# RWKV scans: outputs and next state from one product, its two uses in a step in different PSUM banks, the copy of the outputs later in the order

## The chip, the cores and the metric

The program runs on one core of one Trainium2 chip. A core has five engines that each take their own instructions in order: TensorE (PE, matrix products; its weight loads, PEld, run ahead of the products), VectorE (DVE), ScalarE (ACT), GpSimd (POOL) and SyncE (SP, which only issues DMAs here). They meet at semaphores. Products land in PSUM, which has eight banks; DVE and ACT read them from there. The metric is the device time of one execution in microseconds (us); the time given is the median of several executions.

## What is computed

Two layers of a diffusion backbone: neighbourhood attention and an expert-routed feed-forward layer, then bidirectional RWKV-7 time mixing and a second expert-routed layer, for 512 latent tokens and 256 context tokens of 1024 channels. The change concerns the RWKV scans alone: 16 heads of 64 channels, one scan forward and one backward, each with the 64x64 state S of a head carried from the context tokens into the latent ones. The outputs y of both directions are added.

```python
def _rwkv_step(S, inp):
    r, w, kk, kka, kt, v = inp
    sk = jnp.einsum('bhij,bhj->bhi', S, kk)
    S = S * w[:, :, None, :] - sk[..., None] * kka[:, :, None, :] + v[..., None] * kt[:, :, None, :]
    return S, jnp.einsum('bhij,bhj->bhi', S, r)
...
        S_f, y_f = _rwkv_scan(S0[0], (r, w[0], kk, kk * a[0], kt[0], v), False)
        S_b, y_b = _rwkv_scan(S0[1], (r, w[1], kk, kk * a[1], kt[1], v), True)
        return (S_f, S_b), (y_f + y_b, r, kt, v, g)
```

Everything is float32.

## The kernel before

The kernel goes through four phases in order: attention, first expert layer, RWKV layer, second expert layer. In the RWKV layer the 16 heads are taken in 8 pairs, and each pair has two directions z (0 forward, 1 backward): 16 directions in all. The 768 tokens are 6 tiles m of 128 tokens (0 to 3 latent, 4 and 5 context), each of two chunks u of 64 tokens. A scan does not go token by token: `rw_dir_in` and `rw_invert` turn a chunk into matrices, and `rw_dir_out` then needs one small recurrence per chunk.

For each chunk there is a matrix FT (128 rows; per head 128 columns) and a matrix Z (128 rows; per head 64 columns). Rows 0 to 63 of Z are the chunk's values v, which a DMA brings (`states`); rows 64 to 127 are the state that comes from the chunk before. Columns 64 to 127 of FT give the next state, columns 0 to 63 the chunk's outputs. Of context tiles no outputs are needed.

The functions in `rw_dir_out`, by the order in which `run` calls them for the i-th tile of the direction's order:

- `chain(i, us[0])`: for each of the two heads one product of FT's columns 64 to 127 with Z, into the lower half (partitions 64 to 127) of a tile of the pool `ps_ch`, which has one PSUM bank (tile name `ch`, L1537). DVE multiplies the result by the decay and writes it into the next chunk's Z (L1540).
- `transition(order[i + 1])`: the FT of both chunks of the next tile: products of FR with QF into the pool `ps_mm` (three banks, tile name `mm`, L1520), copied into FT by ACT (L1522) and DVE (L1523, L1527).
- then, after a yield, `chain(i, us[1])`, in the same bank `ch`;
- `solve(order[i + 2])`: products of RHS with TB (L1504), into `mm`, copied into QF by ACT (L1508);
- `outputs(m)`, for latent tiles: four products of FT's columns 0 to 63 with Z, two per chunk, the chunk u in partitions 64u to 64u+63 of one `mm` tile (L1550). For z = 0 ACT copies them to y (tile name `yg`, L1552); for z = 1 DVE adds them to y (L1554).

FT tiles come from the pool `rp`, four in turn. Each product of the program is float32 and shows in the trace as two pairs of LDWEIGHTS and MATMUL, so the two heads of a chain product are x4 in a row of the trace, and the four products of `outputs` are x8.

`weave` sets the order: it runs several generators in turn, one yield of each per step of twelve. In a scan direction's twelve steps stand the `run` of this direction, `rw_dir_in` of the direction four later (transposes L71, products L1380 and their copies BD, BKT, AT, FR, RHS), the decays of the one after (L1298), `rw_join` of the next direction (L1471, L1478), and every second direction the readout of the pair before. Under `manual_schedule` PE, DVE and ACT take the instructions in the order in which the code writes them; the DMAs and POOL's instructions are ordered by a scheduler. After the last `rw_dir_in` the output projection (`fold`, L248 to L250 into `mf`) is laid between the scans' instructions.

`later()` opens the pools `rp`, `jp` and `ro` before the first scan and fills the tiles that stay (E, TB, QF) with zeros.

Of the kernel before, what the change touches and what calls it, by code (L numbers as in the profile page):

```python
# [20 lines left out]
F32 = mybir.dt.float32  # L21
# [4 lines left out]
AF = mybir.ActivationFunctionType  # L26
ALU = mybir.AluOpType
# [4 lines left out]
P = 128  # L32
# [4 lines left out]
NLT = 4  # L37
# [1281 lines left out]
NSP = 3  # L1319
LAG = 4  # L1320
# [164 lines left out]
def rw_dir_out(S, W):  # L1485

    nc = S.nc
# [22 lines left out]
    def transition(m):  # L1510
# [3 lines left out]
        for u in us:  # L1514
# [6 lines left out]
            FT[m][u] = F = S.rp.tile([P, 2, P], F32, name="FT", bufs=4)  # L1521
# [8 lines left out]
    def chain(i, u):  # L1530
        m = order[i]
        c = 2 * m + u
        if u == us[1] and i == NT - 1:
            return
        pz = S.ps_ch.tile([P, 2, 64], F32, name="ch")
        for h in range(2):
            nc.tensor.matmul(pz[64:128, h, :], FT[m][u][:, h, 64:128], Zs[m][:, u, 64 * h:64 * h + 64],  # L1537
                             start=True, stop=True)
        dst = Zs[m][64:128, us[1], :] if u == us[0] else Zs[order[i + 1]][64:128, us[0], :]
        nc.vector.tensor_tensor(dst.rearrange("p (h i) -> p h i", h=2), pz[64:128],  # L1540
                                W.PC[64:128, :, c:c + 1].to_broadcast([64, 2, 64]), op=ALU.mult)

    def outputs(m):
        if m >= NLT:
            return
        po = S.ps_mm.tile([P, P], F32, name="mm")
        for u in range(2):
            for h in range(2):
                r = slice(64 * h, 64 * h + 64)
                nc.tensor.matmul(po[64 * u:64 * u + 64, r], FT[m][u][:, h, 0:64], Zs[m][:, u, r], start=True, stop=True)  # L1550
        if z == 0:
            nc.scalar.activation(y[:, m, :], po, AF.Copy)  # L1552
        else:
            nc.vector.tensor_tensor(y[:, m, :], po, y[:, m, :], op=ALU.add)  # L1554
# [11 lines left out]
    def run():  # L1566
        for i, m in enumerate(order):
            if i + 2 < NT:
                states(order[i + 2])
            chain(i, us[0])  # L1570
            if i + 1 < NT:
                transition(order[i + 1])
            yield
            chain(i, us[1])
            if i + 2 < NT:
                solve(order[i + 2])
            outputs(m)
            yield
# [134 lines left out]
def phase_rw(S):  # L1713
    nc, tc = S.nc, S.tc
    S.rwk = ExitStack()
    with ExitStack() as es:
# [15 lines left out]
        with ExitStack() as e1:  # L1732
# [11 lines left out]
            S.LO, S.TB, S.QF, S.qfi, S.Gs = [], [], [], 0, {}  # L1744
# [15 lines left out]
            def later():  # L1760
# [8 lines left out]
                for z in range(2):  # L1769
# [7 lines left out]
                    S.QF.append(t)  # L1777

# [133 lines left out]
```

## Time and profile before

| | us |
|---|---|
| time, median of 3 runs (lowest, highest) | 2788.53 (2783.61, 2795.34) |
| the profiled execution: its time | 2783.66 |
| the profiled execution: span from the first to the last instruction | 2781.7 |
| PE busy over the span | 2475.8 (89%) |
| DVE busy | 1337.5 (48%) |
| ACT busy | 1004.4 (36%) |
| POOL busy | 595.9 (21%) |

The first `chain` product starts at 1709.3 us of the span and the last scan ends near 2226 us. Before that lie the attention and the first expert layer, the RWKV layer's projections and the filling of its pipeline; after that the second expert layer. Busy is the time in which an engine has at least one instruction under way; PE's products overlap each other and their ends are modelled, so PE can count as busy while it loses time between products. The granted clock (PEclk) is a share of 2.4 GHz: 1.00 is that level, 0.50 is 1.2 GHz.

### The profile page before, as it was taken

How to read it: one execution, taken by the hardware profiler on the slowest of the kernel's cores; microseconds unless marked ns; L12 is line 12 of the kernel's file. 1: busy time of each engine (PE TensorE's matmuls, PEld its weight loads, DVE VectorE, ACT ScalarE, POOL GpSimd, SP SyncE). 2: the span in 40 equal slices, each digit the busy share in tenths (PEclk: the TensorE clock that was granted, in tenths of full speed). 3: DMA queues.
4: the chain of work that ended last, by engine and by line, in shares of the span. 5: the costliest groups of instructions: out<-in, count | busy, mean ns of one | idle time of the engine just before them, and what ended most of it. 6: DMA issues, size and time to landing. Idle time of an engine off the chain costs nothing. (4 is left out here: it accounts for less than half of the span.)

```text
span 2781.7 us, 43985 instructions
## 1 busy us (share of the span) xinstructions
PE 2475.8 (89%) x16803; PEld 1534.7 (55%) x16803; DVE 1337.5 (48%) x2987; ACT 1004.4 (36%) x2121; POOL 595.9 (21%) x855
## 2 busy tenths in 40 slices
PE   6999999889999999997689697999999959988887
PEld 4876778782333322333389596777778843322222
DVE  6656665551222211215978745676676762211221
ACT  3555566531110100113266535676665421000000
POOL 1110000121000000001556535665555200000000
PEclk9999999989999999998899898999999959999999
DMA  8655530329788879774157966556654279999998
GB/s 244 146 157 183 159 114 17 113 103 372 271 345 319 325 287 364 277 292 166 69 176 247 270 158 136 130 127 145 129 115 127 61 274 373 409 409 409 409 409 334
DMA packets 427521, 637.62 MB, mean 229 GB/s; under 512 B 133824, under 2 KB 301056, under 8 KB 427312
## 3 DMA queue, kind: packets, MB, share of 16 engines
q1 hardware_dynamic: 419328, 609.11, 64.7%
q0 software_dynamic: 7984, 25.70, 2.5%
q8 instruction: 134, 2.20, 0.3%
q14 instruction: 75, 0.61, 0.1%
HBM read 565.11 MB, written 53.88 MB: 223 GB/s over the span
## 5 line engine op out<-in xcount | busy, mean ns | idle before, releaser
L759 PE MATMUL P<-wm,xin 128*64 128x512 f32 x2048 | 503.3, 607 | 42.1 <-DMA wm<-in_moe_w_dram 41.9
L759 PEld LDWEIGHTS P<-wm,xin 128*64 128x64 f32 x2048 | 132.8, 137 | 369.8 <-issue 270.8
L792 PE MATMUL mm<-wm,hidT 128*64 128x512 f32 x1024 | 250.8, 601 | 20.4 <-ACT hidT L774 16.1
L768 ACT ACTIVATE hid<-P 128x512 f32<-128x512 f32 x32 | 19.1, 598 | 690.1 <-PE P L759 690.1
L803 DVE SCALAR_TENSOR_TENSOR Y<-mm,gates,gt 64x512 f32<-64x512 f32 x64 | 48.0, 750 | 320.8 <-PE mm L792 320.1
L769 DVE TENSOR_TENSOR hid<-P,hid 128x512 f32<-128x512 f32 x32 | 22.1, 692 | 371.3 <-PE P L759 371.3
L731 POOL DMA_INDIRECT xg<-xnd,ii x20 | 19.1, 956 | 808.1 <-PE tp L71 521.9
L248 PE MATMUL mm<-wh,hTh 128*128 128x256 f32 x576 | 171.6, 298 | 2.5 <-ACT hTh L542 2.5
L250 PE MATMUL mm<-wh,hTl 128*128 128x256 f32 x576 | 166.7, 290 | 1.7 <-DVE hTl L545 1.7
L249 PE MATMUL mm<-wl,hTh 128*128 128x256 f32 x576 | 166.7, 290 | 0.0
L792 PEld LDWEIGHTS mm<-wm,hidT 128*64 128x64 f32 x1024 | 69.0, 136 | 159.5 <-issue 116.4
L763 PE MATMUL Pc<-wm,xin 128*32 128x512 f32 x1024 | 147.3, 602 | 0.0
L1443 POOL TENSOR_TENSOR Wi<-Wi,Ti 112x30 f32<-112x30 f32 (+14 forms) x240 | 142.1, 592 | 18.7
L1441 POOL TENSOR_TENSOR Ti<-Wi 112x30 f32<-112x30 f32 (+14 forms) x240 | 135.8, 566 | 18.2
L248 PEld LDWEIGHTS mm<-wh,hTh 128*128 128x128 f32 x576 | 112.5, 195 | 12.7 <-issue 9.1
L250 PEld LDWEIGHTS mm<-wh,hTl 128*128 128x128 f32 x576 | 112.0, 195 | 4.2 <-DVE hTl L545 2.7
L1520 PE MATMUL mm<-FR,QF 128*128 128x128 f32 (+1 forms) x768 | 113.5, 291 | 0.4 <-ACT QF L1508 0.4
L249 PEld LDWEIGHTS mm<-wl,hTh 128*128 128x128 f32 x576 | 112.6, 196 | 1.4 <-issue 1.4
L830 DVE TENSOR_TENSOR X<-mm,X 128x512 f32<-128x512 f32 x80 | 51.9, 687 | 106.1 <-PE mm L829 105.8
L1520 PEld LDWEIGHTS mm<-FR,QF 128*128 128x128 f32 x768 | 97.1, 197 | 7.4 <-ACT QF L1508 0.9
L1508 ACT ACTIVATE QF<-mm 64x256 f32<-64x256 f32 x192 | 72.9, 379 | 66.8 <-PE mm L1504 63.1
L1523 DVE TENSOR_TENSOR FT<-mm,eye 64x128 f32<-64x128 f32 x192 | 55.9, 292 | 77.4 <-ACT FT L1522 75.4
(429 smaller groups left out, 5697.3 us busy)
## 6 DMA issues: line engine op xcount, KB each, us to landing
wm<-in_moe_w_dram SPq DMA_DIRECT2D x378, 1024.0 KB
adaw<-in_ada_w_dram SPq DMA_DIRECT2D x96, 512.0 KB
wraw<-in_na_w_qkv_dram SPq DMA_DIRECT2D x32, 256.0 KB
wm<-in_moe_w_dram POOLq DMA_DIRECT2D x6, 1024.0 KB, 11.0
pkd<-sig SPq DMA_DIRECT2D x24, 256.0 KB
pkd<-kka SPq DMA_DIRECT2D x24, 256.0 KB
pkd<-av SPq DMA_DIRECT2D x24, 256.0 KB
sig<-pkd SPq DMA_DIRECT2D x16, 384.0 KB
```

The lines of the kernel that those rows point to most:

```text
L248: S.nc.tensor.matmul(ps, xh, wh, start=(k == 0), stop=False)
L249: S.nc.tensor.matmul(ps, xh, wl, start=False, stop=False)
L250: S.nc.tensor.matmul(ps, xl, wh, start=False, stop=(k == n - 1))
L759: nc.tensor.matmul(ps[64 * hf:64 * hf + 64], xin[:, k, cl], w[:, k2, hf * 512:(hf + 1) * 512], start=st, stop=sp)
L763: nc.tensor.matmul(Pc[32 * i:32 * i + 32], xinc[:, k, cc], ws[i // 2][:, k2, (i % 2) * 512:(i % 2 + 1) * 512], start=st, stop=sp)
L792: nc.tensor.matmul(py[64 * hf:64 * hf + 64], hT[:, k % 4, k // 4, :], w[:, k2, hf * 512:(hf + 1) * 512], start=st, stop=sp)
L830: nc.vector.tensor_tensor(X[t][:, sl], ps, X[t][:, sl], op=ALU.add)
L1441: nc.gpsimd.tensor_tensor(t, W3[:, i + 1:32, i:i + 1].to_broadcast([112, n, i]), W3[:, i:i + 1, 0:i].to_broadcast([112, n, i]), op=ALU.mult)
L1443: nc.gpsimd.tensor_tensor(W3[:, i + 1:32, 0:i], W3[:, i + 1:32, 0:i], t, op=ALU.add)
L1508: nc.scalar.activation(QF[m][0:64, u], pq[64 * u:64 * u + 64], AF.Copy)
L1520: nc.tensor.matmul(pf[:, h, s0:], QF[m][:, u, h, :], rhs, start=True, stop=True)
L1523: nc.vector.tensor_tensor(F[64:128, :, 64:128], pf[64:128, :, 64:128], S.eye2[64:128, None, :].to_broadcast([64, 2, 64]), op=ALU.add)
```

## The change

Outputs and next state of a chunk now come from one product. `chain` multiplies all 128 columns of FT with Z, so that the upper half of the PSUM tile (partitions 0 to 63) holds the chunk's outputs and the lower half the next state. `outputs` is gone, with its products. The first chunk of a tile uses the bank `ch`, the second a tile of the pool `ps_mm`. `chain` returns a function that copies the outputs (ACT for z = 0, DVE for z = 1, 64 partitions at a time), and `run` calls it later: for the first chunk behind the instructions of `transition`, for the second behind those of `solve`. The last chunk of a direction, whose state nobody needs, now gets a product for its outputs. Of context tiles the outputs' half is computed too and not read. FT tiles are four fixed tiles of the pool `jp`, which `later()` fills with zeros on DVE, since context tiles leave columns 0 to 63 unwritten.

```diff
--- before.py
+++ after.py
@@ -1317,6 +1317,7 @@
 LATC = 8
 NSET = 5
 NSP = 3
+NFT = 4
 LAG = 4
 LATER, PREP0, PREP, RA, NEXT, NEXT0, RSTART, RRATE, RD = 2, 8, 6, 1.8, 5, 13, 0, 0.6, 1
 
@@ -1518,7 +1521,8 @@
                 r = slice(64 * h, 64 * h + 64)
                 rhs = W.FR[:, c:c + LATC + 1:LATC, r] if lat else W.FR[:, LATC + c, r]
                 nc.tensor.matmul(pf[:, h, s0:], QF[m][:, u, h, :], rhs, start=True, stop=True)
-            FT[m][u] = F = S.rp.tile([P, 2, P], F32, name="FT", bufs=4)
+            FT[m][u] = F = S.FT[S.fti % NFT]
+            S.fti += 1
             nc.scalar.activation(F[0:64, :, s0:], pf[0:64, :, s0:], AF.Copy)
             nc.vector.tensor_tensor(F[64:128, :, 64:128], pf[64:128, :, 64:128],
                                     S.eye2[64:128, None, :].to_broadcast([64, 2, 64]), op=ALU.add)
@@ -1530,28 +1534,26 @@
     def chain(i, u):
         m = order[i]
         c = 2 * m + u
-        if u == us[1] and i == NT - 1:
-            return
-        pz = S.ps_ch.tile([P, 2, 64], F32, name="ch")
+        if u == us[1] and i == NT - 1 and m >= NLT:
+            return lambda: None
+        pool, name = ((S.ps_ch, "ch"), (S.ps_mm, "mm"))[u != us[0]]
+        pz = pool.tile([P, 2, 64], F32, name=name)
         for h in range(2):
-            nc.tensor.matmul(pz[64:128, h, :], FT[m][u][:, h, 64:128], Zs[m][:, u, 64 * h:64 * h + 64],
-                             start=True, stop=True)
-        dst = Zs[m][64:128, us[1], :] if u == us[0] else Zs[order[i + 1]][64:128, us[0], :]
-        nc.vector.tensor_tensor(dst.rearrange("p (h i) -> p h i", h=2), pz[64:128],
-                                W.PC[64:128, :, c:c + 1].to_broadcast([64, 2, 64]), op=ALU.mult)
-
-    def outputs(m):
-        if m >= NLT:
-            return
-        po = S.ps_mm.tile([P, P], F32, name="mm")
-        for u in range(2):
-            for h in range(2):
-                r = slice(64 * h, 64 * h + 64)
-                nc.tensor.matmul(po[64 * u:64 * u + 64, r], FT[m][u][:, h, 0:64], Zs[m][:, u, r], start=True, stop=True)
-        if z == 0:
-            nc.scalar.activation(y[:, m, :], po, AF.Copy)
-        else:
-            nc.vector.tensor_tensor(y[:, m, :], po, y[:, m, :], op=ALU.add)
+            nc.tensor.matmul(pz[:, h, :], FT[m][u][:, h, :], Zs[m][:, u, 64 * h:64 * h + 64], start=True, stop=True)
+        if not (u == us[1] and i == NT - 1):
+            dst = Zs[m][64:128, us[1], :] if u == us[0] else Zs[order[i + 1]][64:128, us[0], :]
+            nc.vector.tensor_tensor(dst.rearrange("p (h i) -> p h i", h=2), pz[64:128],
+                                    W.PC[64:128, :, c:c + 1].to_broadcast([64, 2, 64]), op=ALU.mult)
+
+        def evacuate():
+            if m >= NLT:
+                return
+            o, src = y[64 * u:64 * u + 64, m, :], pz[0:64].rearrange("p h i -> p (h i)")
+            if z == 0:
+                nc.scalar.activation(o, src, AF.Copy)
+            else:
+                nc.vector.tensor_tensor(o, src, o, op=ALU.add)
+        return evacuate
 
     def prepare():
         states(order[0])
@@ -1567,14 +1569,15 @@
         for i, m in enumerate(order):
             if i + 2 < NT:
                 states(order[i + 2])
-            chain(i, us[0])
+            end = chain(i, us[0])
             if i + 1 < NT:
                 transition(order[i + 1])
+            end()
             yield
-            chain(i, us[1])
+            end = chain(i, us[1])
             if i + 2 < NT:
                 solve(order[i + 2])
-            outputs(m)
+            end()
             yield
     return prepare, run
 
@@ -1741,7 +1744,7 @@
                 setattr(S, name, opened(e1, name, b, side="right"))
             S.ps_ch = e1.enter_context(tc.tile_pool(name="ps_ch", bufs=1, space=PSUM))
             S.ps_un = ea.enter_context(tc.tile_pool(name="ps_un", bufs=2, space=PSUM))
-            S.LO, S.TB, S.QF, S.qfi, S.Gs = [], [], [], 0, {}
+            S.LO, S.TB, S.QF, S.qfi, S.FT, S.fti, S.Gs = [], [], [], 0, [], 0, {}
 
             def low(pool, i):
                 t = pool.tile([P, NT, P], F32, name=f"LO{i}")
@@ -1775,6 +1778,10 @@
                     nc.vector.tensor_copy(t[64:128, :, :, 0:64].rearrange("p u h c -> p (u h) c"),
                                           S.eye2[64:128, None, :].to_broadcast([64, 4, 64]))
                     S.QF.append(t)
+                for i in range(NFT):
+                    t = S.jp.tile([P, 2, P], F32, name=f"FT{i}")
+                    nc.vector.memset(t, 0.0)
+                    S.FT.append(t)
 
             def prep(j):
                 yield from rw_join(S, W[j])
```

The order in which the engines get the instructions, at three places. First PE, in a forward direction (z = 0), from a chain product of a context tile to the first one behind the next `outputs` (before):

```order
L1537 MATMUL ch<-Z,FT 64x64 x2
L1520 MATMUL mm<-FR,QF_14658 128x128 x4
L71 MATMUL tp<-ident,kka 128x128 x2
L71 MATMUL tp<-ident,kt 128x128 x2
L1380 MATMUL un<-BD,BKT 128x256 x2
L1537 MATMUL ch<-Z,FT 64x64 x2
L1504 MATMUL mm<-RHS,TB_14651 128x128 x2
L1550 MATMUL mm<-Z,FT 64x64 x4
L71 MATMUL tp<-ident,AT 128x128 x4
L1537 MATMUL ch<-Z,FT 64x64 x2
```

The same place of the changed kernel:

```order
L1542 MATMUL ch<-Z,FT_14661 128x64 x2
L1523 MATMUL mm<-FR,QF_14658 128x128 x4
L71 MATMUL tp<-ident,kka 128x128 x2
L71 MATMUL tp<-ident,kt 128x128 x2
L1381 MATMUL un<-BD,BKT 128x256 x2
L1542 MATMUL mm<-Z,FT_14663 128x64 x2
L1507 MATMUL mm<-RHS,TB_14651 128x128 x2
L71 MATMUL tp<-ident,AT 128x128 x4
L1542 MATMUL ch<-Z,FT_14665 128x64 x2
```

The row of the four outputs' products is gone, the chain products fill 128 partitions instead of 64, every second one goes to `mm`, and nothing else has moved.

Second ACT, in a forward direction, around one `solve` (QF) of a latent tile, before:

```order
L1522 ACTIVATE FT<-mm 64x256 x2
L1371 ACTIVATE BKT<-tp 128x512
L1508 ACTIVATE QF_14653<-mm 64x256 x2
L1552 ACTIVATE yg<-mm 128x128
L1393 ACTIVATE RHS<-tp 128x2x128
L1396 ACTIVATE kt<-tp 128x256
```

And changed:

```order
L1526 ACTIVATE FT_14665<-mm 64x256
L1526 ACTIVATE FT_14667<-mm 64x256
L1553 ACTIVATE yg<-ch 64x128
L1372 ACTIVATE BKT<-tp 128x512
L1511 ACTIVATE QF_14653<-mm 64x256 x2
L1553 ACTIVATE yg<-mm 64x128
L1394 ACTIVATE RHS<-tp 128x2x128
L1397 ACTIVATE kt<-tp 128x256
```

One copy of 128 partitions has become two of 64: one behind the FT copies, and one where the single copy stood, behind the QF copies.

Third DVE, in a backward direction (z = 1), from the first chain product of a latent tile, before:

```order
L1540 TENSOR_TENSOR Z<-ch,PC 64x128
L1523 TENSOR_TENSOR FT<-mm,eye_10602 64x2x64
L1527 TENSOR_TENSOR FT<-mm,AR 64x64 x2
L1523 TENSOR_TENSOR FT<-mm,eye_10602 64x2x64
L1527 TENSOR_TENSOR FT<-mm,AR 64x64 x2
L1381 TENSOR_TENSOR AT<-un,mA_10594 128x2x2x64
L1384 TENSOR_TENSOR FR<-un,mRR_10596 128x256
L1540 TENSOR_TENSOR Z<-ch,PC 64x128
L1554 TENSOR_TENSOR yg<-mm,yg 128x128
```

And changed:

```order
L1545 TENSOR_TENSOR Z<-ch,PC 64x128
L1527 TENSOR_TENSOR FT_14665<-mm,eye_10602 64x2x64
L1531 TENSOR_TENSOR FT_14665<-mm,AR 64x64 x2
L1527 TENSOR_TENSOR FT_14667<-mm,eye_10602 64x2x64
L1531 TENSOR_TENSOR FT_14667<-mm,AR 64x64 x2
L1555 TENSOR_TENSOR yg<-ch,yg 64x128
L1382 TENSOR_TENSOR AT<-un,mA_10594 128x2x2x64
L1385 TENSOR_TENSOR FR<-un,mRR_10596 128x256
L1545 TENSOR_TENSOR Z<-mm,PC 64x128
L1555 TENSOR_TENSOR yg<-mm,yg 64x128
```

The one addition of 128 partitions has become two of 64, the first of them behind the FT instructions and ahead of AT and FR.

## Rows read from the trace of the kernel before

**Rows 1.** Busy time of each engine before, in and after the scans.

```profile
core 0: us, PE busy (x) PEld busy (x) DVE busy (x) ACT busy (x) POOL busy (x), PEclk, DMA share, GB/s
1709.00:2226.00 517.00, 483.86 (x3842) 405.67 (x3842) 359.59 (x1006) 320.09 (x812) 282.62 (x471) 0.98 0.52 118
2226.00:2781.70 555.70, 447.16 (x1947) 167.46 (x1946) 144.15 (x274) 57.62 (x118) 12.05 (x15) 0.94 0.95 379
```

**Rows 2.** One backward direction, cut at starts of chain products; columns of Rows 1.

```profile
1868.90:1876.00 7.10, 6.43 (x51) 5.15 (x50) 5.37 (x10) 5.50 (x14) 6.33 (x10) 1.00 0.42 96
1876.00:1881.50 5.50, 5.50 (x37) 4.51 (x36) 4.40 (x17) 3.15 (x8) 4.03 (x7) 1.00 0.39 104
1881.50:1886.30 4.80, 4.80 (x41) 4.05 (x40) 3.10 (x12) 1.90 (x5) 0.29 (x2) 1.00 1.01 238
1886.30:1891.30 5.00, 5.00 (x41) 4.16 (x41) 3.64 (x10) 2.01 (x5) 0.00 (x0) 1.00 0.65 125
1891.30:1894.50 3.20, 3.20 (x29) 3.08 (x28) 1.32 (x6) 3.14 (x10) 0.00 (x0) 1.00 1.00 240
1894.50:1899.20 4.70, 4.27 (x41) 3.34 (x41) 2.54 (x8) 3.26 (x11) 0.00 (x0) 1.00 1.01 153
```

**Rows 3.** The forward direction behind it, without its last half step.

```profile
1899.20:1906.30 7.10, 6.62 (x51) 5.18 (x51) 5.64 (x12) 5.75 (x15) 2.98 (x8) 1.00 0.65 146
1906.30:1911.80 5.50, 5.50 (x38) 4.50 (x37) 4.02 (x14) 2.89 (x8) 4.72 (x11) 1.00 0.73 133
1911.80:1917.10 5.30, 4.84 (x42) 4.05 (x41) 3.94 (x14) 4.33 (x11) 4.67 (x9) 1.00 0.55 127
1917.10:1922.60 5.50, 5.22 (x41) 4.07 (x40) 4.74 (x14) 3.71 (x8) 4.93 (x8) 1.00 0.08 18
1922.60:1925.80 3.20, 3.20 (x29) 3.08 (x28) 1.30 (x6) 3.14 (x11) 2.85 (x5) 1.00 0.30 56
```

**Rows 4.** Waits in the scans, 1709 to 2226 us: us in total, times, longest us.

```profile
DVE FT L1523 <- ACT FT L1522: 75.4, 98, 2.7
```

**Rows 5.** Timeline of PE's products around one latent step: start us, us, what.

```profile
1886.11 0.28 PE L1380 MATMUL un<-BD,BKT 128*128 128x128 f32 x1
1886.31 0.45 PE L1537 MATMUL ch<-Z,FT 128*64 128x64 f32 x4
1886.69 0.71 PE L1504 MATMUL mm<-RHS,TB 128*128 128x128 f32 x4
1887.33 0.46 PE L1550 MATMUL mm<-Z,FT 128*64 128x64 f32 x8
1887.72 0.66 PE L71 MATMUL tp<-ident,AT 128*128 128x128 f32 x4
1888.21 0.61 PE L1380 MATMUL un<-BD,BKT 128*128 128x128 f32 x4
1888.66 0.59 PE L1298 MATMUL un<-sig,tri 128*128 128x512 f32 x1
```

**Rows 6.** Groups by line, 1709 to 2226 us, shapes apart: busy us, mean ns.

```profile
L1537 PE MATMUL ch<-Z,FT 128*64 128x64 f32 x704 | 79.1, 236 | 12.0 <-DVE Z L1540 9.7 <-ACT QF L1508 0.8 <-ACT foh L240 0.2
...
L1540 DVE TENSOR_TENSOR Z<-ch,PC 64x128 f32<-64x128 f32 x176 | 51.8, 294 | 35.4 <-PE ch L1537 31.9
...
L1522 ACT ACTIVATE FT<-mm 64x128 f32<-64x128 f32 x62 | 16.7, 271 | 29.8 <-PE mm L1520 16.9 <-DVE Z L1540 10.5
```

**Rows 7.** Single lines: the copies of the outputs, and a fill with zeros.

```profile
L1552 ACT ACTIVATE yg<-mm x32: 278/278/280, 1724.9 to 2196.0; 128x128 f32<-128x128 f32 x32
L1554 DVE TENSOR_TENSOR yg<-mm,yg x32: 282/292/293, 1755.1 to 2227.4; 128x128 f32<-128x128 f32 x32
L1774 DVE MEMSET QF<- x2: 485/485/485, 1678.4 to 1681.3; 64x512 f32 x2
```

**Rows 8.** The last half step of two forward directions; columns of Rows 1.

```profile
1865.00:1868.90 3.90, 3.77 (x30) 2.73 (x30) 1.58 (x4) 2.31 (x7) 3.50 (x6) 1.00 0.71 204
1928.80:1935.60 6.80, 6.77 (x31) 4.91 (x31) 1.78 (x4) 2.35 (x7) 5.95 (x11) 0.51 0.58 122
```

## Prediction

> **What bounds the kernel now.** I began with the busy time by phase. In the scans, 1709 to 2226 us, PE is busy 483.86 of 517.00 us, DVE 359.59, ACT 320.09 and POOL 282.62, at a granted clock of 0.98 [rows 1]: the change touches this phase alone, and PE is its fullest engine. What follows hangs on the scans' results and should move along as a whole; DMA is its fullest resource, at 0.95 [rows 1].
>
> A mean hides where PE is really the bound, so I cut two neighbouring directions at the starts of chain products [rows 2, 3]. The reader is to see two kinds of stretch. In some PE fills everything and the others have room: 5.50 of 5.50 us with DVE at 4.40 and 4.02, 4.80 of 4.80 with DVE at 3.10, 5.00 of 5.00 with DVE at 3.64. In others PE has gaps and DVE or ACT come close: 6.43 of 7.10, 4.84 of 5.30, 5.22 of 5.50 (DVE 4.74 there), 4.27 of 4.70; and in 3.20 us both PE and ACT are full (3.14). A PE saving is worth its whole length in the first kind and a part in the second. The list of waits agrees that DVE and ACT mostly wait for what PE started: DVE's FT instructions wait 75.4 us for ACT's FT copies [rows 4], which wait for products.
>
> **The products, on PE.** The timeline of one latent step [rows 5] gives the prices. A product with a 128-wide weight takes 0.11 us a piece there: the four L1380 from 1888.21 to 1888.66 take 0.45. The L1380 that starts at 1886.11 is done with the array at 1886.22; the chain product starts at 1886.31, 0.09 late. It hands over after 0.38 (1886.69), and the four L1504 behind it need 0.64 until 1887.33, where 4 x 0.11 + 0.09 for the next turn to a narrow weight is 0.53: 0.11 more is lost on the way back to the wide weight. So a chain product costs PE 0.09 + 0.38 + 0.10 = 0.57 us, though it holds only four short pieces. From 1886.22 to 1888.21 are 1.99 us; less 8 x 0.11 for L1504 and L71, a chain product and an `outputs` cost 1.10, so `outputs` costs 0.53.
>
> The new product has a full 128-wide weight like its neighbours: no turn, and four pieces at 0.11, that is 0.44 us. No row here prices 64 moving columns behind a wide weight, so I bound it: 0.11 a piece, if the weight sets the pace, or the narrow pieces' spacing, (0.45 - 0.236) / 3 = 0.07 by the x4 row [rows 5] and the mean of one [rows 6]; 0.44 or 0.28 for four. I take 0.44, by the row with the same weight; the other end would save 12 x 0.16 x 16 = 31 us more on PE.
>
> The Trainium skill, "TensorE: Matmul & The Clock Gate", section "LDWEIGHTS (loading the stationary operand)", says that a weight load takes time by its columns, about 1 ns per 1.2 columns; by it alone the wider weight speaks against this change: an estimate from that page is 53 ns per load of 64 columns and 107 of 128, so 176 x 4 + 64 x 8 loads before take 65 us and 768 after 82, and the sum would be 17 us slower. What that leaves out is the turn: the Trainium skill, "TensorEngine Tiling (Array Packing)", section "Key Properties", says that a change of tiling mode drains the engine; the trace shows 0.09 us on the way in and 0.10 on the way out.
>
> Count: L1540, one per chain product, stands x176 [rows 6], so 11 chain products a direction; the output copies stand x32 and x32 [rows 7], so 4 `outputs`. After: 12 products. Per direction 11 x 0.57 + 4 x 0.53 - 12 x 0.44 = 6.27 + 2.12 - 5.28 = 3.1 us, x16 = 50 us. In the last two tiles of a direction there is no `solve` between chain product and `outputs`, so they share turns and the saving is about 0.3 less, x16 = 5. **PE loses 45 us of work.**
>
> **What of it reaches the end.** By stretch, a chain product saves 0.13, an `outputs` 0.53; where PE has gaps I count half. Backward [rows 2]: 1868.90, three chain products, half of 0.39: 0.20. 1876.00, two: 0.26. 1881.50, two and an `outputs`: 0.79. 1886.30, one and one: 0.66. 1891.30: ACT has 3.14 of 3.20, so 0.06. 1894.50, two and two, less the extra product and the shared turns: half of 0.57, 0.28. Sum 2.25 of 30.3 us. Forward [rows 3]: 0.20, 0.26, half of 0.79, half of 0.66 (DVE 4.74 of 5.50), 0.06, and 0.28 for the last stretch: 1.53. With eight directions of each kind: **30 us gained.** The last directions, with the output projection between, are taken as like these.
>
> **The copies.** 32 copies on ACT of 128 partitions at 278 ns and 32 additions on DVE at 292 [rows 7] become 64 and 64 of 64 partitions. The nearest rows are ACT's FT copy from 64 partitions and 128 columns, 271 ns, and DVE's Z multiply from the same tile, 294 ns [rows 6]: a half costs as much as a whole. ACT gets 64 x 0.271 - 32 x 0.278 = 8.4 us more, DVE 64 x 0.294 - 32 x 0.292 = 9.5. DVE's lies in backward directions beside PE-full stretches with DVE at 3.10 and 3.64 of about 5: nothing. If that cover goes, 9.5. ACT's lies in stretches at 2.89 to 4.33 of 5.3 to 5.5 but for one, the forward 3.20 us with ACT at 3.14 [rows 3], where a copy of 0.27 has no room: 8 x 0.27 = 2.2 us lost. If none had room, 8.4.
>
> Behind the first copy ACT has BKT or RHS copies queued, for which PE's products L1380 and `solve` wait; behind the second, RHS and kt. The copy itself waits for its product and, since DVE reads the other half of the bank, stands behind DVE's multiply; the FT copies ahead of it come later than that product by a whole transition. The bank `ch` is next written two chain products on.
>
> **Smaller things.** Four fills of 128x256: a fill of 512 columns took 485 ns [rows 7], so 0.25 each, 1.0 us on DVE, ahead of the RHS of the fourth direction while the pipeline fills. I count all of it; nothing is the other end. PE's last product of a direction, 0.44, is in the sum. POOL's zeroing of a direction's first Z stands five rows later in POOL's order, on an engine busy 282.62 of 517.00 [rows 1], a direction ahead of its use: hidden. The scheduler places some loads of SP differently; no term.
>
> **The clock.** At the end of one forward direction the granted clock is 0.51 and the half step takes 6.80 us; the same one two directions before, at 1.00, takes 3.90 [rows 8]: 2.9 us for one fall from 2.4 to 1.2 GHz. PE is about to have more gaps just there. I count one more fall, 2.9; none or eight (23 us) are the ends.
>
> **Sum.** 30 - 2.2 - 1.0 - 2.9 = 24 us off the profiled execution's 2783.66: 2760. Its span is 2781.7, so 2 us lie around it. The median of the runs, 2788.53, is 4.9 above that execution; I say 2762 for a run of the changed kernel.
>
> **Rivals.** (a) *PE is the bound everywhere*: products wait a bit less behind DVE too, since DVE and ACT start earlier, and nearly all 45 us come through: 2783.66 - 45 + 2.2 + 1.0, about 2742. For it: 483.86 of 517.00. Against: the stretches with gaps. (b) *DVE, ACT or the clock take it back*: DVE's 9.5 and ACT's 8.4 come due, or the clock falls at the end of most forward directions: with the fills 30 - 18 - 1 or 30 - 23 - 1 are left, 2773 to 2778. For it: the forward stretches with DVE 4.74 of 5.50, 5.64 of 7.10. (c) *The turn was no cost of width*: the gaps around narrow products are waits that stay, and only the pieces count: before 11 x 0.28 + 4 x 0.39, after 12 x 0.44, 0.64 more a direction, 10 us slower, 2794. Against: the gaps stand in stretches where PE is full and nobody is late. The Trainium skill's load rule of "TensorE: Matmul & The Clock Gate" would go this way, to the 17 us above. (d) *A new wait at `mm`*, on the other side: banks go round in the order transition, transition, second chain product, `solve`; so the second half of the next transition takes the bank of the second chain product and must wait until its copy, which stands behind the QF copies on ACT, has read it. One such wait in each of 4 latent steps a direction costs 64 waits; the gain is 24 us, so above 0.38 us each the kernel is slower, and at 0.75 it takes 2808. Against: the transition's first half needs the same QF copies, and four pieces, 0.44 us, stand between, for a copy of 0.27.
>
> **Chances.** My forecast (about 14 to 36 us gained) 0.55, (a) 0.17, (b) 0.18, (c) 0.03, (d) 0.07. Range 2738 to 2782: it takes in (a) and (b) and leaves out (c) and (d) with what lies beyond. About 0.5%, 14 us, is what a measurement of this kernel can tell from no change. Faster by more: nearly all of the forecast and (a), 0.70; within: most of (b), (c) and the forecast's edge, 0.22; slower: (d) and a little beside it, 0.08.
>
> **What would show it.** Right: in a row of PE the new product x4 hands over 0.44 us after its start, with no 0.09 ahead; the stretches that were full shrink by 0.26, 0.79 and 0.66; the scans take about 490 us instead of 517; DVE's share rises there. Wrong: PE waiting for ACT or DVE ahead of the second half of a transition (d); a half step with ACT at its whole length and the copy in it (b); more stretches of 0.5 clock (b); products 0.44 long with gaps before them as now (c). The forecast fails too if the earlier parts of the kernel or the last phase move by themselves.

## The result and the profile after

The changed kernel takes **2813.51 us** (median of 5; 2810.58 to 2821.68), the kernel before 2789.39 on the same chip: ratio **1.0094 [1.0075, 1.0112]**. It is slower, outside the range. The profiled execution's span is 2811.7 us at a granted clock of 0.939, against 2781.7 at 0.955.

These two executions differ by 30.0 us, more than the 24.1 of the medians, since the one of the kernel before (2783.66) is among its fastest (2783.61 to 2795.34). To place the 30.0 us I cut both kernels at the start of the first chain product, of the thirteenth direction, and at the last product of the scans. Windows of the kernel before, columns of [rows 1]:

```profile
1709.30:2099.90 390.60, 366.88 (x2868) 302.20 (x2867) 263.06 (x741) 260.25 (x658) 231.80 (x401) 0.98 0.58 128
2099.90:2227.50 127.60, 118.18 (x986) 104.63 (x986) 97.18 (x268) 59.85 (x154) 51.25 (x72) 0.97 0.32 87
```

Windows of the changed kernel: the same two; a backward direction from its second stretch on, answering to [rows 2]; the forward direction behind it, answering to [rows 3] and, in its last two rows, to the end of a direction in [rows 8]; and the place where the clock falls at that end:

```profile
1713.00:2129.90 416.90, 384.44 (x2532) 344.11 (x2530) 266.86 (x765) 265.83 (x682) 224.51 (x399) 0.89 0.56 121
2129.90:2265.00 135.10, 118.41 (x884) 111.63 (x883) 101.31 (x281) 60.69 (x164) 54.19 (x76) 0.93 0.29 81
...
1964.90:1970.70 5.80, 5.51 (x40) 5.09 (x38) 4.37 (x17) 3.26 (x8) 0.00 (x0) 1.00 0.85 189
1970.70:1975.30 4.60, 4.16 (x33) 3.82 (x32) 3.32 (x13) 1.89 (x5) 0.20 (x1) 1.00 0.83 187
1975.30:1980.00 4.70, 4.70 (x35) 3.83 (x33) 4.04 (x12) 1.86 (x5) 0.00 (x0) 1.00 0.97 172
1980.00:1983.20 3.20, 3.20 (x30) 3.15 (x29) 1.17 (x5) 3.14 (x10) 0.00 (x0) 1.00 0.40 57
1983.20:1988.10 4.90, 4.31 (x30) 3.62 (x30) 3.25 (x11) 3.41 (x11) 1.84 (x7) 1.00 0.78 175
...
1988.10:1995.20 7.10, 6.26 (x51) 5.55 (x51) 5.90 (x12) 5.65 (x15) 6.37 (x10) 1.00 0.41 66
1995.20:2000.80 5.60, 5.47 (x38) 5.08 (x37) 3.99 (x13) 2.65 (x7) 4.97 (x9) 1.00 0.51 106
2000.80:2006.40 5.60, 4.47 (x34) 4.02 (x34) 3.44 (x11) 4.59 (x13) 4.91 (x10) 1.00 0.31 86
2006.40:2012.50 6.10, 5.19 (x35) 3.78 (x33) 5.34 (x16) 3.43 (x10) 5.53 (x8) 1.00 0.07 16
2012.50:2016.40 3.90, 3.34 (x30) 3.10 (x29) 1.21 (x5) 3.84 (x13) 3.45 (x6) 1.00 0.27 52
2016.40:2020.10 3.70, 2.75 (x19) 2.15 (x18) 2.83 (x8) 3.11 (x9) 3.27 (x6) 1.00 0.65 137
2020.10:2025.00 4.90, 4.90 (x18) 3.90 (x19) 1.15 (x3) 2.26 (x7) 4.09 (x11) 0.53 0.73 161
...
2016.90:2020.40 3.50, 2.55 (x17) 1.95 (x17) 2.66 (x6) 2.91 (x10) 3.11 (x6) 1.00 0.55 103
2020.40:2030.60 10.20, 10.20 (x44) 9.17 (x44) 4.54 (x10) 4.49 (x12) 5.55 (x11) 0.50 0.63 163
```

The first twelve directions lost 26.3 us (416.9 against 390.6), the last four 7.5; the scans began 3.7 later, and what follows them was 7.5 shorter (546.7 against 554.2). 26.3 + 7.5 + 3.7 - 7.5 = 30.0. The column to read is the clock: a stretch of length L at mean clock c holds 2 x (1 - c) x L of half clock, 15.6 us in the first twelve directions before and 91.7 after (c has two digits, so within about 4). The last rows show one fall: PE busy 2.55 of 3.50 us, then 10.2 us at 0.50 in which PE is busy all the time. In these twelve directions the changed kernel's clock falls nine times, each time between a direction's ninth chain product and its end, and stays low for 3.4 to 13.7 us; in the kernel before it falls twice, for 6.8 and 10.2 us. At full clock the stretches did not shrink either: the backward ones have the same sum as before, the forward ones are 1.7 us longer (5.60, 5.60, 6.10, 3.90 for 5.50, 5.30, 5.50, 3.20).

Waits of the changed kernel in the scans (us, times, longest):

```profile
DVE FT L1527 <- ACT FT L1526: 91.6, 103, 2.6
...
ACT yg L1553 <- DVE Z L1545: 18.5, 23, 3.1
...
PE mm L1507 <- DVE FT L1531: 9.1, 17, 2.9
```

The first answers to [rows 4], 75.4 us. The other two are new: the copy of the outputs waits for DVE's multiply of the same tile, and `solve` waits for DVE's part of FT. The timelines show what they look like (start, us, what, idle before), first PE's wait at `mm` in the stretch of 5.80 us; then PE around a second product, which answers to [rows 5]; then ACT, PE behind it in the next half step, and PE at the end of that direction, ahead of the fall at 2020.4:

```profile
1964.96 0.56 PE L1542 MATMUL mm<-Z,FT 128*128 128x64 f32 x4
1965.81 0.68 PE L1507 MATMUL mm<-RHS,TB 128*128 128x128 f32 x4 [0.29 <-DVE FT L1531]
...
1974.93 0.61 PE L1381 MATMUL un<-BD,BKT 128*128 128x128 f32 x4
1975.37 0.56 PE L1542 MATMUL mm<-Z,FT 128*128 128x64 f32 x4
1975.77 0.66 PE L1507 MATMUL mm<-RHS,TB 128*128 128x128 f32 x4
...
2008.15 0.78 ACT L1511 ACTIVATE QF<-mm 64x256 f32<-64x256 f32 x2 [1.31 <-PE mm L1507]
2010.23 0.27 ACT L1553 ACTIVATE yg<-mm 64x128 f32<-64x128 f32 x1 [1.29 <-DVE Z L1545]
2010.52 0.38 ACT L1394 ACTIVATE RHS<-tp 128x256 f32<-128x256 f32 x1
...
2012.50 0.64 PE L1542 MATMUL ch<-Z,FT 128*128 128x64 f32 x4
...
2015.08 0.30 PE L1479 MATMUL mm<-T,E 128*128 128x32 f32 x1 [0.56 <-ACT E L1475]
...
2017.83 0.49 PE L1507 MATMUL mm<-RHS,TB 128*128 128x128 f32 x2 [0.76 <-ACT TB L1482]
2018.51 0.49 PE L1507 MATMUL mm<-RHS,TB 128*128 128x128 f32 x2 [0.19 <-ACT TB L1482]
```

ACT idles 1.29 us with RHS and more queued behind the copy, and in the next half step PE waits 0.56 for ACT. The product itself is as forecast: it begins 0.44 behind four pieces of 0.11, without a turn, and hands over after 0.40.

### The profile page after: what moved, and what is told of

Read it like the earlier page. It is cut to its first block, busy times and chain, and to the rows that moved or that the text cites. A ratio compares the mean times of both kernels' runs of the same rounds, so it can differ in the third digit from the quotient of the medians.

```text
span 2811.7 us, 43331 instructions
## 1 busy us (share of the span) xinstructions
PE 2488.8 (89%) x16355; PEld 1579.4 (56%) x16355; DVE 1344.7 (48%) x3023; ACT 1008.5 (36%) x2153; POOL 589.6 (21%) x855
## 5 line engine op out<-in xcount | busy, mean ns | idle before, releaser
L1523 PE MATMUL mm<-FR,QF 128*128 128x128 f32 (+1 forms) x768 | 120.6, 307 | 0.5 <-ACT QF L1511 0.3
L1523 PEld LDWEIGHTS mm<-FR,QF 128*128 128x128 f32 x768 | 109.4, 219 | 1.3 <-ACT QF L1511 0.9
```

Source lines behind the costliest of these rows:

```text
L1523: nc.tensor.matmul(pf[:, h, s0:], QF[m][:, u, h, :], rhs, start=True, stop=True)
```

## The experiments

For every run: its time against the kernel before, and the window of its profiled execution over the first twelve directions with the half clock that this row's mean holds. Times of before on the same chips were 2784.9 to 2789.4 us. This table is the main measurement.

| run | us | ratio to before | twelve directions, us | clock | half clock, us |
|---|---|---|---|---|---|
| before | 2789.39 | | 390.6 | 0.98 | 15.6 |
| the change | 2813.51 | 1.0094 [1.0075, 1.0112] | 416.9 | 0.89 | 91.7 |
| e1_swap | 2800.60 | 1.0070 [1.0043, 1.0097] | 404.3 | 0.94 | 48.5 |
| e2_ring | 2780.81 | 0.9988 [0.9970, 1.0006] | 393.9 | 0.96 | 31.5 |
| e3_tp | 2812.05 | 1.0096 [1.0067, 1.0124] | 415.8 | 0.91 | 74.8 |
| e4_one | 2818.36 | 1.0134 [1.0099, 1.0169] | 425.1 | 0.90 | 85.0 |
| e5_dve | 2815.87 | 1.0091 [1.0064, 1.0118] | 423.3 | 0.87 | 110.1 |
| e6_fwd0 | 2806.43 | 1.0059 [1.0034, 1.0084] | 411.4 | 0.90 | 82.3 |
| e7_first | 2816.54 | 1.0118 [1.0088, 1.0147] | 417.6 | 0.89 | 91.9 |
| e8_swapdve | 2793.38 | 1.0018 [0.9999, 1.0038] | 398.8 | 0.93 | 55.8 |
| e9_nooutputs | 2789.21 | 0.9995 [0.9977, 1.0014] | 405.1 | 0.88 | 97.2 |
| e10_wide | 2793.21 | 1.0009 [0.9989, 1.0029] | 400.4 | 0.94 | 48.0 |
| e11_fill | 2812.58 | 1.0086 [1.0056, 1.0115] | 403.1 | 0.99 | 8.1 |
| e12_fillafter | 2815.72 | 1.0091 [1.0064, 1.0118] | 405.9 | 0.99 | 8.1 |
| e13_fillfwd | 2793.40 | 1.0033 [1.0018, 1.0048] | 393.0 | 0.95 | 39.3 |
| e14_fillmid | 2808.65 | 1.0076 [1.0059, 1.0094] | 419.1 | 0.92 | 67.1 |
| e15_ra | 2807.38 | 1.0087 [1.0059, 1.0115] | 411.3 | 0.96 | 32.9 |
| e16_swapra | 2803.74 | 1.0056 [1.0038, 1.0075] | 410.8 | 0.94 | 49.3 |
| e17_thinend | 2795.72 | 1.0033 [1.0021, 1.0045] | 416.5 | 0.87 | 108.3 |
| e18_thinmid | 2787.72 | 0.9998 [0.9983, 1.0014] | 407.8 | 0.90 | 81.6 |

The last three columns are of one execution each. Against them stands the half clock of whole executions, the scans and all the rest, from the mean clock and the span of each. Its median is 267 us in the kernel before (86 executions, 222 to 307), 337 in the change, 293 in e8_swapdve, 320 in e9_nooutputs, 258 in e11_fill, 259 in e12_fillafter, 292 in e14_fillmid, 318 in e17_thinend and 298 in e18_thinmid. The large differences of the table stand; those of some 30 us could be chance. Among the 86 executions of the kernel before, on five chips, time rises with half clock by 0.26 us for each us, by a straight line through the distances from each chip's mean.

**First theory: the ring of `mm` (R).** R says that the order in which tiles take the banks makes `solve` wait. Three banks go round as T0, T1 (the two chunks of a transition), second chain product, `solve`, so `solve` takes T0's bank of its own step and waits for the FT copies. Before, it took that of the `outputs` of the step before.

e1_swap:

```diff
-        pool, name = ((S.ps_ch, "ch"), (S.ps_mm, "mm"))[u != us[0]]
+        pool, name = ((S.ps_mm, "mm"), (S.ps_ch, "ch"))[u != us[0]]
-            end = chain(i, us[0])
+            chain(i, us[0])()
```

> Changed kernel with the two products' banks exchanged: the first product of a step takes `mm`, the second takes `ch`, and the first's copy stands right behind its multiply, so that the banks of `mm` go round as first product, T0, T1, solve. Theory R (ring): the loss comes from `solve` taking T0's bank of the same step; here `solve` takes the first product's bank, long free, T0 and T1 take banks of the step before, and the time falls below 2784 us, about 2760, with few stretches of half clock in the scans. Rival C (the clock falls because PE has less work in a step, whatever the ring): the work is the same, so 2800 to 2815 us and as many half-clock stretches as the changed kernel. Rival A (the late copies on ACT that wait for DVE's multiply): the first copy still waits there, now ahead of the FT copies, so 2810 us or more. Rival W (128-wide product slower by itself): no change, 2810 us.

e2_ring, in the kernel before:

```diff
             chain(i, us[1])
+            outputs(m)
             if i + 2 < NT:
                 solve(order[i + 2])
-            outputs(m)
```

> The kernel before with `outputs` called ahead of `solve` in a step, nothing else: its banks of `mm` go round as T0, T1, outputs, solve, so `solve` takes T0's bank of the same step, as in the changed kernel; the narrow products, the one copy a tile and PE's work stay. R: 2800 to 2830 us, slower than before, with PE or ACT's QF waiting in the latent steps and more stretches of half clock. C, A and W: nothing of theirs is in it, so 2780 to 2797 us; `outputs` ahead of `solve` puts at most 16 x 4 x 0.53 = 34 us of PE's work ahead of `solve`, most of it not on the path.

e3_tp (second product in `S.ps_tp`) and e4_one (both products in `S.ps_ch`, both copies right behind the product):

```diff
-        pool, name = ((S.ps_ch, "ch"), (S.ps_mm, "mm"))[u != us[0]]
+        pool, name = ((S.ps_ch, "ch"), (S.ps_tp, "tp"))[u != us[0]]
```

> Changed kernel with the second product of a step in a bank of `tp` (the pool of the transposes, two banks) in place of `mm`; the copies stand late as in the change. The banks of `mm` go round as T0, T1, solve, so `solve` takes the bank of T0 of the step before... three allocations a step, each takes its own kind's bank of the step before, all long read. R: clearly faster than the changed kernel, 2765 to 2790 us, less whatever the products of `tp` now wait for. C, A and W: 2805 to 2815 us, as the changed kernel.

> Changed kernel with both products of a step in the one bank `ch`, each copied right behind its multiply. The banks of `mm` go round as T0, T1, solve. R: 2765 to 2795 us; the second product now waits on PE for the first's copy, which is early, so little. Rival A: the copies on ACT stand ahead of the FT and QF copies and wait for the multiply, 2815 us or more. C and W: 2805 to 2815 us.

R falls as the cause of the loss: the ring alone, in the kernel before, costs nothing (0.9988), and two kernels without it are as slow as the change. Only the exchange gained some, and it also moved a copy.

**Second theory: the late copies (A2).** The wait of 18.5 us for DVE's multiply.

e5_dve copies the forward outputs on DVE (the diff); e6_fwd0 leaves them out (`if m >= NLT or z == 0: return`, y filled with zeros); e7_first writes the forward `nc.scalar.activation` ahead of the multiply in `chain`; e8_swapdve is e1_swap with the diff of e5_dve:

```diff
-                nc.scalar.activation(o, src, AF.Copy)
+                nc.vector.tensor_copy(o, src)
```

> Changed kernel with the output copies of the forward directions on DVE in place of ACT, at the same place in the order. Theory A2 (the copy on ACT waits for DVE's multiply of the same bank, which stands behind other work of DVE, and holds up all that is queued on ACT behind it; the waits list of the changed kernel has 18.5 us of it in the scans, and the forward directions are where the time was lost): that wait is gone, since both stand on DVE; the half step that took 6.1 to 6.6 us in the forward directions takes 5.6 or less, and the time falls to 2780 to 2795 us with fewer half-clock stretches. Theory R (solve takes T0's bank): unchanged, 2805 to 2815 us. Rival C (clock falls by PE's lighter work alone): 2805 to 2815 us.

> Changed kernel without the output copies of the forward directions: y is filled with zeros on POOL instead, so the forward directions' part of the outputs is left out. A2: the most that the copies can have cost, 2765 to 2785 us, at or under the kernel before. R and C: 2800 to 2812 us, since the ring and PE's work stay; only 8.4 us of copies leave ACT.

> Changed kernel with the forward directions' ACT copy ahead of DVE's multiply instead of behind it: the copy waits for its product alone, the multiply waits for the copy. A2: ACT is not held up any more, DVE's multiply is later by at most a copy (0.27 us) where ACT is late; 2785 to 2805 us. R and C: 2805 to 2815 us. If the copies' place behind other ACT work then holds up the multiply, and with it the recurrence, 2815 us or more.

> The kernel with the two products' banks exchanged (first product in `mm`, second in `ch`), and the forward copies on DVE too. A2 with R: both waits gone, 2755 to 2775 us, below the kernel before. A2 alone (the ring is nothing): the same as with the copies on DVE in the changed kernel. C: about 2800 us, as with the exchange alone.

A2 falls as the main cause: without any forward copy the kernel still takes 1.0059. In e7_first the wait is only turned round: DVE's multiply waits for ACT's copy, 40.2 us in 28 places. The copies do cost a place: in e6_fwd0 the two stretches that took 6.10 and 3.90 us in the change take, at full clock,

```profile
1867.60:1873.50 5.90, 5.22 (x34) 3.81 (x34) 5.23 (x15) 3.44 (x7) 5.35 (x8) 1.00 0.07 15
1873.50:1876.70 3.20, 3.20 (x30) 3.15 (x30) 1.23 (x5) 3.14 (x11) 2.81 (x6) 1.00 0.26 46
```

0.20 and 0.70 less. And in e8_swapdve the backward stretches that answer to 5.80, 4.60, 4.70 and 3.20 in the change read

```profile
1952.10:1957.30 5.20, 5.20 (x38) 4.89 (x37) 4.21 (x16) 2.87 (x7) 0.00 (x0) 1.00 0.88 205
1957.30:1961.80 4.50, 4.25 (x35) 3.94 (x33) 3.48 (x13) 1.89 (x5) 0.20 (x1) 1.00 0.75 146
1961.80:1966.20 4.40, 4.40 (x34) 3.82 (x33) 3.62 (x11) 1.97 (x5) 0.00 (x0) 1.00 1.25 232
1966.20:1969.80 3.60, 3.31 (x30) 3.14 (x29) 1.91 (x8) 3.51 (x10) 0.00 (x0) 1.00 0.68 87
```

so the wait at `mm` costs up to 0.6 us in the first (the timeline above shows 0.29 of idle time for it); the best arrangement is level with the kernel before (1.0018), not under it.

**Third theory: PE's clock (C).** Two runs on the side of the kernel before. e9_nooutputs drops `outputs` (`if m >= 0: return`), e10_wide makes the chain product alone 128 wide and keeps `outputs`:

```diff
-            nc.tensor.matmul(pz[64:128, h, :], FT[m][u][:, h, 64:128], Zs[m][:, u, 64 * h:64 * h + 64],
-                             start=True, stop=True)
+            nc.tensor.matmul(pz[:, h, :], FT[m][u][:, h, :], Zs[m][:, u, 64 * h:64 * h + 64], start=True, stop=True)
```

> The kernel before without `outputs`: the 64 product groups on PE and the 64 copies are left out, y is filled with zeros on POOL, so the scans' outputs are left out. The copies did not cause the loss (without those of the forward directions the changed kernel still took 2806 us). Theory C: the loss comes from PE's clock, which falls at the end of a direction when PE has less to do there; the changed kernel has some 106 us of half clock in the scans, the kernel before 24. C expects here more half clock than in the kernel before, and 2765 to 2800 us, at most a small part of the 64 x 0.53 = 34 us that leave PE. Without C, a kernel in which PE is nearly full and loses 34 us of work, and ACT and DVE 18 us of copies, is faster by 20 us or more: 2755 to 2768 us, with 24 us of half clock.

> The kernel before with the chain product alone made 128 wide (its upper half, the output, is computed and not used); the narrow `outputs` and their copies stay, and the FT tiles are the changed kernel's four fixed ones. Rival W (the wide product is slower by itself, or the wait is in the FT ring): 2800 us or more. C and A2: PE loses 11 x 0.13 = 1.4 us a direction and no stretch at the end of a direction loses an `outputs`, so 2770 to 2795 us and some 24 to 50 us of half clock.

The window of e9_nooutputs:

```profile
1705.40:2110.50 405.10, 377.37 (x2483) 315.00 (x2482) 262.79 (x717) 256.55 (x634) 230.29 (x403) 0.88 0.57 123
```

34 us of PE's work and 64 copies are gone, and the time is the same (0.9995); half clock is six times that of before, without any wait of the change in it. The wide product by itself is no loss (1.0009).

Then PE got unused work in the changed kernels: e11_fill on e8_swapdve and e12_fillafter on the change, at the end of every direction; e14_fillmid on e8_swapdve, as many pieces in the middle (`1 <= i < 4`, none at `solve`); e13_fillfwd on e8_swapdve, only the pieces at `solve`, and only where a forward direction ends. A product is two pieces, so the 12 products of a direction are 24 pieces: x2820 in the window of e12_fillafter against x2532 in that of the change are 288 more in twelve directions, 31.7 us at 0.11. The expectations count 12 pieces and 21 us in all (e13_fillfwd: 4 and 3.5), half of what was put in.

```diff
         pz = pool.tile([P, 2, 64], F32, name=name)
+        for h in range(2 if i >= 4 else 0):
+            nc.tensor.matmul(pz[:, h, :], S.ident, S.ident[:, 0:64], start=True, stop=True)
...
-    def solve(m):
+    def solve(m, fill=0):
         pq = S.ps_mm.tile([P, 2, P], F32, name="mm")
+        for h in range(fill):
+            nc.tensor.matmul(pq[:, h % 2, :], S.ident, S.ident, start=True, stop=True)
...
-        solve(order[0])
+        solve(order[0], 2)
```

> The kernel with banks exchanged and forward copies on DVE (2793 us), plus work for PE that nobody uses: two products of identity by identity ahead of each of the next direction's first two `solve`, and two of 64 columns ahead of each chain product of a direction's last two tiles, into the same tile, which the true product then overwrites; 12 pieces a direction, 16 x 12 x 0.11 = 21 us of PE in all. C: the end of a direction is dense again, half clock in the scans falls from some 85 us to under 40, and the time to 2765 to 2785 us although PE has more to do. If the clock is only a sign and not the cause, the added work costs up to its 21 us: 2793 to 2814 us.

> The changed kernel with the same unused products added. C: less half clock than its 106 us and 2780 to 2805 us; less is regained than with the banks exchanged, since the added products wait for the same bank as `solve` here. If the clock is only a sign: 2813 to 2835 us.

> The kernel with banks exchanged and forward copies on DVE, plus unused products at fewer places: two of identity by identity ahead of each of the first two `solve` of the next direction, at the ends of the forward directions alone (4 pieces, 8 directions, 3.5 us of PE in all). Over the first twelve directions the kernels so far took 379 to 390 us plus about 0.37 us for each us of half clock. C: if these pieces fall into the wait of PE that stands ahead of the drop, half clock there goes from 55 us to 30 or less, and the time from 2793 to 2780 to 2788 us. If they are too few, 2790 to 2797 us.

> The same base with as many unused pieces as the run with 12 a direction, but in the middle of a direction (two ahead of each chain product of its second to fourth tile), where PE is full. C: the end of a direction stays thin, so half clock in the scans stays at 50 to 75 us, and the pieces cost their whole 16 x 12 x 0.11 = 21 us: 2808 to 2820 us. If any added work held the clock, half clock falls under 40 us as it did with the pieces at the end.

Windows of e11_fill, of e12_fillafter and of e14_fillmid:

```profile
1720.40:2123.50 403.10, 372.17 (x2819) 340.07 (x2818) 283.67 (x813) 257.53 (x634) 226.47 (x391) 0.99 0.59 121
```

```profile
1716.00:2121.90 405.90, 373.81 (x2820) 339.08 (x2819) 270.13 (x765) 266.51 (x682) 227.79 (x404) 0.99 0.60 125
```

```profile
1711.90:2131.00 419.10, 397.73 (x2820) 366.60 (x2819) 283.80 (x813) 258.21 (x634) 224.89 (x400) 0.92 0.55 120
```

At the end the pieces hold the clock (0.99); in the middle they do not (0.92). e11_fill and e14_fillmid have the same base and the same number of pieces, and in the first twelve directions differ by 16.0 us and 59.0 us of half clock: 0.27 us for each. This takes the pieces to cost the same at both places, which is not shown. C's expectations of the whole times failed, and those of e11_fill and e12_fillafter lie where I had put a clock that is only a sign; so the whole times do not decide, the first twelve directions do. On e8_swapdve the pieces at the end cost more than the clock gave back (403.1 us against 398.8), and the last four directions took 142.5 us in both runs with pieces at every end, 137.4 in e13_fillfwd and 130.7 in e14_fillmid, so that as a whole e14_fillmid is no slower than e11_fill. Its 2808.65 us lie in the expected range by luck: twice the work went in, and some 16 us came out (1.0076 against 1.0018). In the last four directions e13_fillfwd shows a wait for a load of the output projection, with a scan's copies queued behind it on ACT:

```profile
ACT foh L240 <- DMA fraw<-od: 7.6, 1, 7.6
```

e15_ra and e16_swapra spread the preparation of a later direction towards the end instead, on the change and on e8_swapdve:

```diff
-LATER, PREP0, PREP, RA, NEXT, NEXT0, RSTART, RRATE, RD = 2, 8, 6, 1.8, 5, 13, 0, 0.6, 1
+LATER, PREP0, PREP, RA, NEXT, NEXT0, RSTART, RRATE, RD = 2, 8, 6, 1.4, 5, 13, 0, 0.6, 1
```

> The changed kernel with the preparation of a later direction woven in at 1.4 of its steps a half step instead of 1.8, so that it reaches to the last half steps of a direction, where PE was thin; no work is added or left out. C: half clock in the scans falls from 107 us to under 60 and the time to 2785 to 2805 us. If the clock is only a sign, or the preparation's own order matters more: 2805 to 2825 us.

> The kernel with banks exchanged and forward copies on DVE, and the preparation at 1.4 steps a half step. C: half clock under 40 us in the scans and 2765 to 2785 us, below the kernel before. If the weave's rate hurts elsewhere (the copies of the preparation come due in the last half steps, where ACT and DVE have their own): 2790 to 2805 us.

Half clock fell to 32.9 us in e15_ra, but the twelve directions still took 411.3, and the whole times of e15_ra and e16_swapra lie where the rivals of C expected them: the new order costs time of its own. From the second to the tenth direction e15_ra's forward directions take 34.6 us on average where the change's take 38.2, and its backward ones 35.1 for 31.9; why, is not settled.

Last, the kernel before without half of its `outputs`: those of a direction's last two tiles (e17_thinend; e18_thinmid has `i >= 4`, the other two).

```diff
-            outputs(m)
+            if i < 4:
+                outputs(m)
```

> The kernel before without `outputs` in the last two tiles of each direction (32 of 64 product groups, 17 us of PE, and their copies are left out; y is filled with zeros on POOL). C: the thin end alone makes the clock fall: half clock in the scans 70 us or more where the kernel before has 25, and 2785 to 2805 us, no faster than the kernel before although 17 us of PE and 9 us of copies are gone. Without C: 2770 to 2780 us and 25 us of half clock.

> The kernel before without `outputs` in the other two latent tiles, those of a direction's middle; as many are left out. C: the end stays as it was, half clock stays at 25 to 45 us, and PE's 17 us come through in part: 2770 to 2782 us, below the run with the same left out at the end by 8 us or more. If any less work lowers the clock: as that run.

Their windows, e17_thinend, then e18_thinmid:

```profile
1708.80:2125.30 416.50, 391.93 (x2675) 326.59 (x2674) 264.64 (x729) 258.43 (x646) 227.36 (x409) 0.87 0.55 122
```

```profile
1707.90:2115.70 407.80, 382.72 (x2676) 317.53 (x2675) 263.93 (x729) 259.54 (x646) 230.77 (x405) 0.90 0.56 123
```

With none of the change in it, 17 us less work at the end make the kernel slower, 1.0033 [1.0021, 1.0045]. The same work taken from the middle makes it no faster; there I had expected the clock to stay, and half clock is 81.6 us: less work in the middle lowers the clock too, though by less. All seven falls of e18_thinmid still begin between a direction's ninth and eleventh chain product, where no work had been left out. The two differ by 8.7 us and 26.7 us of half clock, 0.33 us for each.

## Why the prediction was wrong

**"The clock" is the step that failed.** It counted one more fall, 2.9 us, with eight (23 us) as the far end. There are 76 us more of half clock in twelve directions, nine falls instead of two. At 0.27 (e11_fill against e14_fillmid) to 0.33 (e17_thinend against e18_thinmid) that is an estimated 20 to 25 us of the 26.3 lost; the 0.26 among the executions of the kernel before agrees. Over whole executions the medians differ by 70 us of half clock, 18 to 23 of the 24.1 us. The direct test agrees in its sign: e12_fillafter is the change with the clock held, and its twelve directions take 11.0 us less although 31.7 us of pieces came in, so the clock was worth 11.0 or more there; how much more is not shown, since pieces may have filled waits. My price of a fall was rather high (2.9 us for a fall of 6.8, 0.43 us for each us of half clock), and the count far too low: the ends of the directions were already where the clock fell at times [rows 8], and half of the `outputs` that the change removes stood there. Rival **(b)** had this mechanism as one of its ways, with eight falls and 23 us, and more stretches of 0.5 clock as its sign; I gave it 0.18 in all, and it too kept the 30 us gained.

**"What of it reaches the end" failed as well**, the 30 us. Without the 20 to 25 us for the clock, the change still loses 1 to 6 us in twelve directions, where I had a gain of 22.5. In a backward direction, at full clock, the stretches gave 0.30 lost, 0.20, 0.30, 0 gained and 0.20 lost where I had 0.26, 0.79, 0.66, 0.06 and 0.28 gained. Where PE saves time, the next wait takes it: for the bank of `mm` (5.80 with it, 5.20 without), for ACT behind the late copy (3.90 with, 3.20 without). Even in e8_swapdve, without those, the four stretches shrink from [rows 2]'s 18.50 to 17.70, by 0.80 of the 1.77 forecast.

**"The products, on PE"** held: no turn ahead of the product, 0.40 for four pieces. Rival (c) is not borne out: the wide product alone gives 1.0009 [0.9989, 1.0029]. Nor is the loss of 17 us that I had estimated from the load rule of the Trainium skill, "TensorE: Matmul & The Clock Gate", section "LDWEIGHTS (loading the stationary operand)".

**"The copies"**: the prices held (ACT 268 ns, DVE 283 ns for a half, by the durations of L1553 and L1555), and DVE's additions cost nothing that I could see. ACT's was under-sized: I had the copy standing behind DVE's multiply, and did not price the wait, 18.5 us in 23 places. Rival **(d)** named a wait at `mm` but at another place, and took it for the whole; the ring alone costs nothing in the kernel before (0.9988).

Of the rest, 7.5 us in the last four directions, up to 4 can be the clock (0.93 against 0.97: 11 us more of half clock); what remains is open. Open too is how much of the added half clock comes from the work that left PE and how much from the new waits: e1_swap, without the wait of `solve` for DVE's FT, and e8_swapdve, without that and the copy's, have about half of it, while e9_nooutputs, with none of the change's waits, has as much in the table as the change.

No version here beats the kernel before; the best is level with it.

## What to carry to other kernels

Before work is taken from PE, look at the granted clock of every stretch and at where it already falls now and then: work that leaves a thin stretch can cost more in clock than it saves (e17_thinend), and work that leaves the middle can lower the clock at the end (e18_thinmid). Price a saving on PE by its stretches at either clock level, and test it by leaving the work out altogether: e9_nooutputs would have told in one run that there was nothing to gain. In these kernels a tile that two engines read makes the second in the program's order wait for the first (18.5 us here, 40.2 the other way round in e7_first); if the first stands far back in its engine's order, all that is queued behind the second waits too.

## What the runs showed of the hardware that was not expected

Less work on PE made a kernel slower, with nothing else changed but its copies and a fill with zeros on POOL (e17_thinend, 1.0033 [1.0021, 1.0045]). The Trainium skill, "TensorE: Matmul & The Clock Gate", section "HAM oscillation — how this bites in real kernels", tells of falls behind long waits for DMA; here the clock falls behind short gaps: in the 3.50 us ahead of the fall at 2020.4 us, PE's waits are 0.76 and 0.19, both for ACT (the timeline above). The same page of the Trainium skill, section "A second HAM failure mode: psum-queue depth-cycling", says that frequent short idle times between groups of products, in a kernel that goes round PSUM banks, do it as well; this fall agrees.
